# State's update by two additions over pairs of heads, and the last phase's projection weights split once and kept

## The chip, the cores and the metric

The kernel runs on one core of a Trainium2 chip. The metric is the device time of one execution in microseconds. Before the change it is 3080.32 us, the median of three runs (3077.19 to 3084.64).

Of the core's engines, the kernel uses TensorE (PE in the profile; PEld are its weight loads) for all matrix products, VectorE (DVE), ScalarE (ACT) and GpSimd (POOL) for the elementwise work, and SyncE (SP) to issue nearly all DMAs. Each engine works through its own queue in order; semaphores tie the queues together.

## The reference

One decoder block on x of 2048 tokens by 1024 channels, all in float32. A normalized and modulated input h goes through one wide projection. Its columns feed two mixers, both of which run causally over the tokens: a conv branch (gated, a depthwise convolution 31 wide, a layer norm, swish) and a rwkv branch with a matrix state of 64 x 64 for each of 16 heads. Both are gated, projected (w_conv_out, w_rwkv_out), merged by sigmoid gates, projected again (w_out), added to x and normalized.

```python
def step(state, inp):
    r_t, w_t, k_t, v_t, kk_t, b_t = inp
    sk = jnp.einsum('bhvk,bhk->bhv', state, kk_t)
    state = (state * w_t[:, :, None, :] - sk[..., None] * b_t[:, :, None, :]
             + v_t[..., None] * k_t[:, :, None, :])
    return state, jnp.einsum('bhvk,bhk->bhv', state, r_t)
...
h = _rmsnorm(x, norm_g[l]) * (1.0 + scale[:, None, :]) + shift[:, None, :]
p = jnp.einsum('bsd,de->bse', h, w_in[l])
...
m = jax.nn.sigmoid(g_conv) * y_conv + jax.nn.sigmoid(g_rwkv) * y_rwkv
out = jnp.einsum('bsd,de->bse', m, w_out[l])
x = x + gate[:, None, :] * out
```

## The kernel before

**Products by splitting.** Each large product takes float32 operands apart into a rounded high half (`hi`) and the rest (`lo`), and adds up three matmuls: hi x hi, hi x lo, lo x hi (`mm3`, L192). A weight tile is 1024 x 128, or 512 KB. `load_w` brings it in: either it loads the float32 tile (L172), rounds it on ACT (L175) and subtracts on DVE or POOL (L177), or, if both halves were written to DRAM before (`kept`), it loads the two halves (L168, L169), 512 KB each. All these tiles come from one pool of six buffers. The input projection's weights are split in the first block of tokens and kept. The weights of w_out, multiplied by the adaLN gate, are split and kept in the second block: `ogate`, by half tiles, with scratch tiles from a pool of eight (`hx`), ACT at L157 and POOL at L156 and L158. The weights of w_rwkv_out (`ro`) and w_conv_out (`co`) are not kept: `rproj` and `cproj` of the last phase load and split all eight tiles of each again for each block, on ACT and DVE.

**Stages.** The tokens run in four blocks of 512 (block 0 to 3). In each, four groups of two pairs of heads go through `group`; between its steps stand the projections for the conv branch and for the gates, each with its matmuls against h. A last phase then takes block by block: `rproj`, `cproj`, and the output projection with the residual and the final norm. For the block after, `osplit` and `lnorm` prepare the inputs: `m` or `o` tiles (hi and lo) for `rproj`, `u` tiles for `cproj`. `lnorm` ends in u on the path POOL L1024, ACT, DVE L202, DVE L1026, ACT and DVE in `split` (L911, L912).

**The state.** A block has 8 chunks of 64 tokens. A pair's step (`pair`, a generator in three parts) writes `BK`, which holds beta (L499, DVE) and k (L505, POOL) divided by the running decay, and `KR`, which holds the removal key and r times it. L518 copies BK by heads and L524 multiplies the copies with KR for the matrices within a chunk; L555 transposes BK and L556 copies it as `tk`. `pe` is the chunk's whole decay, one number for each channel and chunk. In `group`, for each chunk: ACT makes Se = S x pe (L665); TensorE applies S (L668), DVE adds (L670), TensorE solves within the chunk (L673), DVE scales (L675), TensorE sums tk with the result (L679), and DVE makes the new S as pe times that sum plus Se (L683), for two pairs by two heads in four operations of 64 x 64.

**What sets the order.** Everything is written with tiles whose waits are worked out by the language, and the instructions are put in order, on each engine and across them, by a scheduler that plays through its own estimate of each instruction's time. So an edit in one place can move instructions far from it. BK has one buffer, `tk` three, KR four.

Of the kernel before, what the change touches and what calls it, by code (L numbers as in the profile page):

```python
# [9 lines left out]
F32 = mybir.dt.float32  # L10
F32R = mybir.dt.float32r
# [7 lines left out]
P = 128  # L19
# [63 lines left out]
def hybrid_block(ctx: ExitStack, tc: tile.TileContext, x, vecs, convk, w2a2, final_g, ada, w_in, w_co, w_ro, w_o, crow, out,  # L83
# [63 lines left out]
    def ogate(n, half):  # L147

        back = kept.setdefault(("o", n), [dp.tile([P, KT, P], F32R, name=f"k{p_}_o{n[0]}_{n[1]}", tag=f"k{p_}_o{n[0]}_{n[1]}")
                                          for p_ in "hl"])  # L150
        hs = slice(half * 4, half * 4 + 4)
        st, gr, hi, lo = hx("w_st"), hx("w_gr"), hx("w_hi"), hx("w_lo")
        nc.sync.dma_start(st.rearrange("p (k n) -> p k n", k=4), wsrc["o"][n][:, hs, :])
        nc.sync.dma_start(gr[:, :256], grow_d[n[0] * 256:n[0] * 256 + 256].unsqueeze(0).broadcast_to([P, 256]))
        s4 = st.rearrange("p (k n) -> p k n", n=256)
        nc.gpsimd.tensor_tensor(out=s4, in0=s4, in1=gr[:, :256].unsqueeze(1).broadcast_to([P, 2, 256]), op=ALU.mult)  # L156
        nc.scalar.copy(hi.bitcast(F32R), st)  # L157
        nc.gpsimd.tensor_tensor(out=lo.bitcast(F32R), in0=st, in1=hi, op=ALU.subtract)  # L158
        for d_, s_ in zip(back, (hi, lo)):
            nc.sync.dma_start(d_[:, hs, :].bitcast(F32), s_.rearrange("p (k n) -> p k n", k=4))  # L160
# [283 lines left out]
    def pair(b, q_, pr, h, lora, uv, Asb, rn, res):  # L444
# [102 lines left out]
        nc.gpsimd.tensor_tensor(out=vv, in0=rk, in1=vv, op=ALU.mult)  # L547
        nc.sync.dma_start(bv_dram[b][pr], vv)

        tk = l3.tile([P, NCH, P], F32, name="tk", tag="tk", bufs=TKB)  # L550
        for c4 in range(NCH // 4):
            pt = pa.tile([P, 4, P], F32, name="aux", tag="aux")
# [7 lines left out]
    def group(b, g, h, lora, fill):  # L560
# [98 lines left out]
        for c in range(NCH):  # L659
# [18 lines left out]
            for q in range(2):  # L678
                last = nc.tensor.matmul(xo[:, 2 + q, :], R[q]["tk"][:, c, :], uv[:, c, q, :], start=False, stop=(q == 1),  # L679
                                        skip_group_check=True)  # L680
            for q, hh in heads:
                hs = slice(64 * hh, 64 * hh + 64)
                nc.vector.scalar_tensor_tensor(out=Sg[hs, q, hs], in0=xo[hs, 2 + q, hs],  # L683
                                               scalar=R[q]["pe"][hs, c:c + 1], in1=Se[hs, q, hs],
                                               op0=ALU.mult, op1=ALU.add)

        O = XO[:, 0::2]
        for c4 in range(NCH // 4):
# [170 lines left out]
    for b in range(NB):  # L859
        h = hprep(b) if b else hprep0(x0, ada_steps())  # L860
        lora = lora_split(h)
        for g in groups:
# [11 lines left out]
            if b == 1:  # L874
                for _ in range(2):
                    n_ = later.pop(0)
                    for half in range(2):
                        ogate(n_, half)

            def fill(step, n=None):  # L880
                for _ in range(n or (FILL0[step] if b == 0 and g == 0 else 0)):
# [257 lines left out]
```

## Time and profile before

| | us |
|---|---|
| median of three runs | 3080.32 |
| the profiled execution | 3079.25 |
| its span, first to last instruction | 3077.6 |
| TensorE busy in the span | 2918.8 |
| DVE busy | 2182.2 |
| POOL busy | 1161.0 |
| ACT busy | 1059.7 |
| bytes moved | 638.41 MB, mean 207 GB/s |

The four blocks of tokens run from 0 to about 650, 1235, 1830 and 2425 us, and the last phase from there. A row of stretches gives the stretch and its length, the busy time of PE, PEld, DVE, ACT and POOL with the number of instructions, the granted TensorE clock, the busy share of the DMA engines, and GB/s. A row of groups gives line, engine, operation, out<-in, shapes and count, then busy time and mean ns, and then idle time of the engine just before, with what ended it. A row of one line or tile gives shortest, median and longest duration in ns, and the first and last start. A row of waits gives who waited for what: us in total, times, longest. A row of the timeline gives start, duration and in brackets the idle time before. A row of DMA issues ends in KB each and the median us to landing.

### The profile page before, as it was taken

To read this page: it belongs to the slowest core of one execution; us is meant where nothing else is said; L and a number is where in the kernel's file an instruction comes from. 1 tells how busy PE (TensorE), PEld (TensorE's weight loads), DVE (VectorE), ACT (ScalarE), POOL (GpSimd) and SP (SyncE) were. 2 spreads that over 40 slices of the span, in tenths; PEclk is the share of its full clock that TensorE was granted. 3 is DMA by queue.
4 is the path that set the end of the run, shared out by engine and by line. 5 is a ranking of instruction groups with operands and counts; after the bars stand their busy time and mean duration, and the time that the engine had idled before them with its cause. 6 is when DMAs were issued, how large, how long until landed. Compare 5 with 4: busy or idle time off the path is not lost.

```text
span 3077.6 us, 64859 instructions
## 1 busy us (share of the span) xinstructions
PE 2918.8 (95%) x25672; PEld 2759.5 (90%) x25672; DVE 2182.2 (71%) x4199; ACT 1059.7 (34%) x1919; POOL 1161.0 (38%) x1724
## 2 busy tenths in 40 slices
PE   6799998999999999999999999999989999699998
PEld 5789998999999999999999998999989888487888
DVE  7677877787777667777768586867699465877553
ACT  4424444343324241424232323233342224343421
POOL 3355554534343434241323326345445016533100
PEclk9989999999999999999999999999989999799999
DMA  8675767664757586555646567647448658766554
GB/s 301 221 239 192 262 206 268 229 235 136 249 160 229 163 269 218 178 167 173 204 149 217 181 202 247 192 142 224 139 146 263 207 187 287 246 205 220 198 182 161
DMA packets 343327, 638.41 MB, mean 207 GB/s; under 512 B 133424, under 2 KB 152176, under 8 KB 343024
## 3 DMA queue, kind: packets, MB, share of 16 engines
q1 hardware_dynamic: 343024, 634.27, 62.8%
q8 instruction: 202, 3.31, 0.4%
q14 instruction: 101, 0.83, 0.1%
HBM read 462.10 MB, written 170.92 MB: 206 GB/s over the span
## 4 chain that ended last, share of the span: by engine, by line
PE 62%; DVE 12%; DMA 10%; POOL 7%; issue 3%; ACT 2%; SPq 2%; DVEq 0%; POOLq 0%; ACTq 0%
PE ps_main L192 43%; PE aux L524 3%; DVE acc L761 2%; DMA w_st<-w_in_t 2%; POOL TT L611 2%; POOL itmp L609 2%; PE xo L673 2%; PE pout L1061 2%; PE pout L1060 2%; PE pout L1059 2%; DMA w_lo<-kl_in 1%; PE xo L668 1%; DMA w_gr<-grow_d 1%; PE xo L679 1%; PE late L695 1%
## 5 line engine op out<-in xcount | busy, mean ns | idle before, releaser
L192 PE MATMUL ps_main<-h_hi,w_hi 128*128 128x256 f32 x4608 | 961.4, 286 | 20.4 <-ACT w_hi L175 12.2
L192 PE MATMUL ps_main<-h_hi,w_lo 128*128 128x256 f32 x4608 | 962.3, 286 | 13.6 <-POOL w_lo L177 8.0
L192 PE MATMUL ps_main<-h_lo,w_hi 128*128 128x256 f32 x4608 | 956.7, 285 | 0.0
L192 PEld LDWEIGHTS ps_main<-h_hi,w_hi 128*128 128x128 f32 x4608 | 721.7, 190 | 30.4 <-ACT w_hi L175 13.3
L192 PEld LDWEIGHTS ps_main<-h_hi,w_lo 128*128 128x128 f32 x4608 | 719.7, 190 | 21.6 <-POOL w_lo L177 10.0
L192 PEld LDWEIGHTS ps_main<-h_lo,w_hi 128*128 128x128 f32 x4608 | 719.8, 190 | 5.2 <-issue 0.5
L761 DVE SCALAR_TENSOR_TENSOR acc<-u,ck,acc 128x512 f32<-128x512 f32 x928 | 698.6, 753 | 20.0
L175 ACT CAST w_hi<-w_st 128x1024 fp32r<-128x1024 f32 x135 | 141.5, 1048 | 368.9 <-DMA w_st<-w_in_t 151.6
L683 DVE SCALAR_TENSOR_TENSOR S<-xo,pe,Se 64x64 f32<-64x64 f32 x512 | 144.6, 282 | 128.1 <-PE xo L679 118.1
L609 POOL TENSOR_TENSOR itmp<-La,TT 128x126 f32<-128x126 f32 (+22 forms) x496 | 180.7, 364 | 141.9 <-DMA La<-dA 105.9
L611 POOL TENSOR_TENSOR TT<-TT,itmp 128x126 f32<-128x126 f32 (+22 forms) x496 | 190.5, 384 | 37.2
L177 DVE TENSOR_TENSOR w_lo<-w_st,w_hi 128x1024 fp32r<-128x1024 f32 x88 | 119.5, 1359 | 103.7 <-ACT w_hi L175 47.7
L177 POOL TENSOR_TENSOR w_lo<-w_st,w_hi 128x1024 fp32r<-128x1024 f32 x47 | 113.5, 2414 | 134.5 <-ACT w_hi L175 109.0
L665 ACT ACTIVATE Se<-S,pe 128x128 f32<-128x128 f32 x256 | 89.0, 395 | 209.1 <-DVE S L683 208.0
L524 PE MATMUL aux<-KR,BKz 128*128 128x128 f32 x1024 | 138.5, 285 | 13.5 <-ACT BKz L518 8.7
L547 POOL TENSOR_TENSOR vv<-rk,vv 128x512 f32<-128x512 f32 x32 | 44.0, 1374 | 284.2 <-ACT rk L546 268.8
L524 PEld LDWEIGHTS aux<-KR,BKz 128*128 128x128 f32 x1024 | 127.6, 198 | 16.1 <-ACT BKz L518 9.1
L675 DVE TENSOR_TENSOR uv<-xo,rn 64x256 f32<-64x256 f32 x128 | 53.7, 420 | 99.8 <-PE xo L673 98.2
L741 ACT ACTIVATE th<-ps_main 128x512 f32<-128x512 f32 x64 | 38.1, 595 | 210.5 <-PE ps_main L192 157.6
L526 DVE TENSOR_TENSOR As<-aux,maskA 128x512 f32<-128x512 f32 x128 | 87.0, 688 | 27.9 <-PE aux L524 26.4
L451 POOL TENSOR_TENSOR wlo<-wf,wl 64x128 fp32r<-64x128 f32 x64 | 37.4, 584 | 173.6 <-ACT wl L448 171.1
L773 ACT ACTIVATE th<-ps_main 128x512 f32<-128x512 f32 x64 | 38.2, 597 | 184.3 <-PE ps_main L192 179.7
(298 smaller groups left out, 5489.0 us busy)
## 6 DMA issues: line engine op xcount, KB each, us to landing
w_hi<-kh_in SPq DMA_DIRECT2D x219, 512.0 KB, 4.0
w_lo<-kl_in SPq DMA_DIRECT2D x219, 512.0 KB, 5.1
w_st<-w_in_t SPq DMA_DIRECT2D x73, 512.0 KB, 5.0
kh_in<-w_hi SPq DMA_DIRECT2D x71, 512.0 KB, 2.9
kl_in<-w_lo SPq DMA_DIRECT2D x71, 512.0 KB, 4.4
w_st<-w_ro_t SPq DMA_DIRECT2D x32, 512.0 KB, 4.0
w_st<-w_co_t SPq DMA_DIRECT2D x32, 512.0 KB, 3.6
w_hi<-kh_o SPq DMA_DIRECT2D x32, 512.0 KB, 3.7
```

The lines of the kernel that those rows point to most:

```text
L175: nc.scalar.copy(hi, st)
L177: lo_eng.tensor_tensor(out=lo, in0=st, in1=hi.bitcast(F32), op=ALU.subtract)
L192: nc.tensor.matmul(ps[:, qs], ww[:, k, :], aa[k][:, qs], start=(k == 0 and t == 0 and q == 0), stop=(k == KT - 1 and t == 2 and q == ms - ...
L524: nc.tensor.matmul(pA[:, c // 2, es], BKz[:, hh, c // 2, es], KR[:, cc, es], start=(c == 0), stop=(c == 3), skip_group_check=True)
L526: nc.vector.tensor_tensor(out=Asb[:, hh, c4 * 4:c4 * 4 + 4, :].rearrange("p (a e) n -> p a (e n)", e=2), in0=pA, in1=flat(maskA).unsqueeze ...
L609: nc.gpsimd.tensor_tensor(out=tmp[:, :ni, :nt], in0=La[:, j:j + 1, j + 1:].broadcast_to([P, ni, nt]), in1=TT[:, :ni, j:j + 1].broadcast_to ...
L611: nc.gpsimd.tensor_tensor(out=TT[:, :ni, j + 1:], in0=TT[:, :ni, j + 1:], in1=tmp[:, :ni, :nt], op=ALU.add)
L665: nc.scalar.mul(Se[:, q, :], Sg[:, q, :], R[q]["pe"][:, c:c + 1])
L673: nc.tensor.matmul(xo[pr_, q, hs], As[q][pr_, hh, c, kcol(e)], XO[pr_, c, q, hs], start=(q == 0 and hh == 0), stop=(q == 1 and hh == 1), s ...
L683: nc.vector.scalar_tensor_tensor(out=Sg[hs, q, hs], in0=xo[hs, 2 + q, hs], scalar=R[q]["pe"][hs, c:c + 1], in1=Se[hs, q, hs], op0=ALU.mult ...
L761: nc.vector.scalar_tensor_tensor(out=acc if i + 1 < HALO else yj, in0=u[:, i:i + TB], scalar=ck[:, j, i:i + 1], in1=acc, op0=ALU.mult, op1 ...
L1059: nc.tensor.matmul(o_, mhi[kk][:, ts_], whi[:, k, :], start=first, stop=False, skip_group_check=True)
```

## The change

Three edits. First, after BK's last use within a chunk and before its transposes, one POOL multiplication scales all of BK (128 x 1024) by pe, so that `tk` already holds the decay. Second, the new state is then the plain sum of Se and TensorE's result, and one DVE addition serves both pairs: two operations of 64 x 128 for each chunk instead of four of 64 x 64. Third, `keep` splits the 16 tiles of w_rwkv_out and w_conv_out in block 2, four tiles at the start of each group, by half tiles on ACT and POOL like `ogate`, and stores both halves; `load_w` finds them in `kept` and loads the halves in the last phase.

```diff
+    pending = [(name, n) for name in ("ro", "co") for n in range(KT)]
+
+    def keep(name, n, half):
+        back = kept.setdefault((name, n), [dp.tile([P, KT, P], F32R, name=f"k{p_}_{name}{n}", tag=f"k{p_}_{name}{n}")
+                                           for p_ in "hl"])
+        hs = slice(half * 4, half * 4 + 4)
+        st, hi, lo = hx("w_st"), hx("w_hi"), hx("w_lo")
+        nc.sync.dma_start(st.rearrange("p (k n) -> p k n", k=4), wsrc[name][n][:, hs, :])
+        nc.scalar.copy(hi.bitcast(F32R), st)
+        nc.gpsimd.tensor_tensor(out=lo.bitcast(F32R), in0=st, in1=hi, op=ALU.subtract)
+        for d_, s_ in zip(back, (hi, lo)):
+            nc.sync.dma_start(d_[:, hs, :].bitcast(F32), s_.rearrange("p (k n) -> p k n", k=4))
...
+        BKe = BK.rearrange("p a (e n) -> p (a e) n", e=2)
+        nc.gpsimd.tensor_tensor(out=BKe, in0=BKe, in1=pe.unsqueeze(2).broadcast_to([P, NCH, 2 * CH]), op=ALU.mult)
         tk = l3.tile([P, NCH, P], F32, name="tk", tag="tk", bufs=TKB)
...
-            for q, hh in heads:
+            for hh in range(2):
                 hs = slice(64 * hh, 64 * hh + 64)
-                nc.vector.scalar_tensor_tensor(out=Sg[hs, q, hs], in0=xo[hs, 2 + q, hs],
-                                               scalar=R[q]["pe"][hs, c:c + 1], in1=Se[hs, q, hs],
-                                               op0=ALU.mult, op1=ALU.add)
+                nc.vector.tensor_tensor(out=Sg[hs, :, hs], in0=xo[hs, 2:4, hs], in1=Se[hs, :, hs], op=ALU.add)
...
+            if b == 2:
+                for _ in range(4):
+                    n_ = pending.pop(0)
+                    for half in range(2):
+                        keep(*n_, half)
```

The scheduler puts the whole program in a new order; lines of the changed kernel are 13 to 18 higher than those of the one before. Three places.

SP's queue in the last phase, at block 0's `rproj`; `rth` is a tile of the gate. Before:

```order
L172 DMA w_st<-w_ro_t 128x1024
L959 DMA rth<-gr_d_2_261 128x512
L959 DMA rth<-gr_d_3_262 128x512
L172 DMA w_st<-w_ro_t 128x1024 x2
L959 DMA rth<-gr_d_4_263 128x512
L172 DMA w_st<-w_ro_t 128x1024
```

In the changed kernel:

```order
L181 DMA w_hi<-kh_ro_16159 128x1024
L182 DMA w_lo<-kl_ro_16160 128x1024
L977 DMA rth<-gr_d_2_261 128x512
L181 DMA w_hi<-kh_ro_17986 128x1024
L182 DMA w_lo<-kl_ro_17987 128x1024
L977 DMA rth<-gr_d_3_262 128x512
L181 DMA w_hi<-kh_ro_18006 128x1024
L182 DMA w_lo<-kl_ro_18007 128x1024
```

Each tile is now two loads of the same size, with nothing of ACT or DVE behind them.

DVE's queue in the last phase, where block 1's `lnorm` works out its scale (`rv`, `dg`), with the low halves of block 2's o tiles and block 0's final norm (`xt`, `vs`, `rs`) beside it. Before:

```order
L130 SCALAR_TENSOR_TENSOR rv<-rt,rv 128x4
L177 TENSOR_TENSOR w_lo<-w_st,w_hi 128x1024
L912 TENSOR_TENSOR o_lo_33076<-ot,o_hi_33077 128x512
L1013 TENSOR_SCALAR dg<-ident,rv 128x128 x4
L912 TENSOR_TENSOR o_lo_33074<-ot,o_hi_33075 128x512
L1067 TENSOR_TENSOR xt_31909<-pout,xt_31909 128x256
L1067 TENSOR_TENSOR xt_31913<-pout,xt_31913 128x256
L1074 TENSOR_REDUCE vs<-sq_31923 128x1
L1075 TENSOR_SCALAR vs<-vs 128x1
L177 TENSOR_TENSOR w_lo<-w_st,w_hi 128x1024
```

In the changed kernel:

```order
L1085 TENSOR_TENSOR xt_31985<-pout,xt_31985 128x256
L130 SCALAR_TENSOR_TENSOR rv<-rt,rv 128x4
L128 TENSOR_TENSOR rs_t<-rs_32463 128x1
L130 SCALAR_TENSOR_TENSOR rs_32482<-rs_t,rs_32482 128x1
L1031 TENSOR_SCALAR dg<-ident,rv 128x128 x4
L129 SCALAR_TENSOR_TENSOR rs_t<-rs_t,vs 128x1
L128 TENSOR_TENSOR rs_t<-rs_32482 128x1
L130 SCALAR_TENSOR_TENSOR rs_32463<-rs_t,rs_32463 128x1
L129 SCALAR_TENSOR_TENSOR rs_t<-rs_t,vs 128x1
L128 TENSOR_TENSOR rs_t<-rs_32463 128x1
```

The two weight subtractions are gone from here, and steps of block 0's final norm stand in their place around `dg`.

POOL's queue in block 0, the scaling of a pair's BK; `s_lo` belongs to the head sums, `vv` to the bonus output, `ta` to the next pair. Before:

```order
L271 TENSOR_TENSOR s_lo<-rk,rh 128x512
L472 COPY pe<-E_4871 128x8
L177 TENSOR_TENSOR w_lo<-w_st,w_hi 128x1024
L547 TENSOR_TENSOR vv<-rk,vv 128x512
L177 TENSOR_TENSOR w_lo<-w_st,w_hi 128x1024
L503 TENSOR_TENSOR ta<-ta,k 128x512
```

In the changed kernel:

```order
L485 COPY pe<-E_4843 128x8
L564 TENSOR_TENSOR BK<-BK,pe 128x1024
L190 TENSOR_TENSOR w_lo<-w_st,w_hi 128x1024
L560 TENSOR_TENSOR vv<-rk,vv 128x512
L190 TENSOR_TENSOR w_lo<-w_st,w_hi 128x1024
L516 TENSOR_TENSOR ta<-ta,k 128x512
```

The scaling stands ahead of a weight split of the first block, of `vv` and of the next pair's work.

## The prediction

> **What bounds the kernel now.** I read the busy shares first, then the same shares by stage: the four token blocks (0, 650, 1235, 1830 us) and the last phase from 2425.
>
> ```profile
> PE 2918.8 (95%) x25672; PEld 2759.5 (90%) x25672; DVE 2182.2 (71%) x4199; ACT 1059.7 (34%) x1919; POOL 1161.0 (38%) x1724
> 0.00:650.00 650.00, 578.19 (x5284) 556.17 (x5285) 478.64 (x904) 260.63 (x439) 309.79 (x425) 0.96 0.71 239
> ...
> 1235.00:1830.00 595.00, 590.65 (x5752) 574.93 (x5751) 434.76 (x884) 197.00 (x377) 186.05 (x365) 1.00 0.57 183
> 1830.00:2425.00 595.00, 579.10 (x5634) 558.86 (x5633) 439.99 (x835) 189.67 (x339) 269.44 (x421) 0.98 0.61 196
> 2425.00:3078.00 653.00, 596.03 (x3386) 511.39 (x3385) 401.18 (x721) 213.51 (x382) 171.11 (x116) 0.95 0.63 210
> ```
>
> TensorE bounds the four blocks: in block 2 it idles 4 us of 595. The change takes no matmul away, so only its idle time and its slow-clock time can be won, and most of those lie in the last phase. Cutting that phase finer finds the place.
>
> ```profile
> 2550.00:2575.00 25.00, 20.68 (x148) 19.73 (x148) 10.62 (x19) 6.96 (x17) 16.92 (x14) 0.86 0.97 356
> 2575.00:2600.00 25.00, 25.00 (x214) 25.00 (x214) 11.89 (x25) 9.60 (x25) 19.69 (x15) 1.00 0.81 271
> 2600.00:2625.00 25.00, 14.84 (x70) 11.30 (x68) 24.72 (x45) 10.11 (x19) 20.58 (x15) 0.90 0.49 166
> 2625.00:2650.00 25.00, 23.72 (x94) 18.93 (x95) 24.95 (x43) 14.97 (x21) 10.32 (x5) 0.89 0.97 335
> 2650.00:2675.00 25.00, 10.99 (x31) 7.69 (x30) 21.22 (x24) 3.75 (x5) 15.12 (x11) 0.72 0.84 266
> 2675.00:2700.00 25.00, 19.76 (x62) 14.56 (x62) 12.44 (x14) 7.90 (x11) 14.45 (x10) 0.73 0.50 160
> ```
>
> From 2600 to 2675 DVE is full (24.7, 25.0 and 21.2 us of each 25) while TensorE idles and its granted clock (third column from the right) drops to 0.72. This is block 1's pair of projections, rwkv then conv. TensorE's waits in 2600 to 2700, and the rows that bracket them:
>
> ```profile
> PE ps_main L192 <- DVE rs L125: 10.8, 1, 10.8
> PE ps_main L192 <- ACT w_hi L175: 10.8, 2, 6.2
> PE ps_main L192 <- DVE w_lo L177: 8.5, 3, 4.1
> 2604.34 0.39 PE L192 MATMUL ps_main<-m_lo,w_hi 128*128 128x512 f32 x1
> 2623.72 1.21 DVE L177 TENSOR_TENSOR w_lo<-w_st,w_hi 128x1024 fp32r<-128x1024 f32 x1
> 2626.84 0.63 PE L192 MATMUL ps_main<-m_lo,w_hi 128*128 128x512 f32 x1
> 2627.27 0.63 PE L192 MATMUL ps_main<-m_hi,w_lo 128*128 128x512 f32 x1
> L1059 PE MATMUL pout<-w_hi,m_hi x256: 277/281/283, 2737.7 to 3066.4; 128*128 128x256 f32 x128
> 2932.28 89.61 PE ps_main L192 x384
> ```
>
> The two projections run from 2604.0, one matmul before the fourth row, to 2737.7, where the output projection's first matmul of the m tiles stands: 133.7 us. The last row, from the chain of waits, is block 3's pair: the same 384 matmuls without a wait in 89.6 us, 0.233 apart; after a stall they start 0.43 apart (the rows at 2626.84 and 2627.27). Of the 44 us between, 30.1 are the waits above, all for weight splits: I count the 10.8 under "rs" too, since w_lo stood in DVE's queue behind those square-root steps and ended at 2624.9. The remaining 14 are mostly the slow clock.
>
> **Part 1, the kept weights, last phase.** Per projection tile, 64 times, ACT's rounding and DVE's subtraction go away and a 512 KB load becomes two.
>
> ```profile
> L175 ACT CAST w_hi<-w_st 128x1024 fp32r<-128x1024 f32 x135 | 141.5, 1048 | 368.9 <-DMA w_st<-w_in_t 151.6 <-DMA w_st<-w_co_t 84.3 <-DMA w_st<-w_ro_t 66.3
> L177 DVE TENSOR_TENSOR w_lo<-w_st,w_hi x88: 1209/1225/2364, 91.2 to 3010.5; 128x1024 fp32r<-128x1024 f32 x88
> L177 DVE TENSOR_TENSOR w_lo<-w_st,w_hi 128x1024 fp32r<-128x1024 f32 x7 | 9.6, 1368 | 0.0
> L912 DVE TENSOR_TENSOR u_lo<-y,u_hi x8: 677/682/1699, 2632.5 to 2670.7; 128x512 fp32r<-128x512 f32 x8
> ```
>
> 64 x 1.05 = 67 us of ACT and 64 x 1.225 = 78 us of DVE, by the median, leave. What is late next is the conv projection's input u, whose last low half starts at 2670.7 and ends at 2672.4. The third row is the DVE subtractions between 2598 and 2671, seven, 9.6 us, ahead of it in a full queue. So u is whole at about 2662.8, and the rwkv projection, no longer waiting, ends at 2604 + 44.8 = 2649. The conv projection's first tile waits for u, its other seven need 7 x 24 x 0.233 = 39.2, and that wait costs some 3.5 of slow clock (14 us of wait, after which about 7 run at half speed): it ends at 2662.8 + 1 + 39.2 + 3.5 = 2706.5 instead of 2737.7, a gain of 31. Bounds: 22 if u comes no earlier (2672.4 + 1 + 39.2 + 3.5 = 2716), 43 if u is never waited for (2604 + 89.6 + 1.5 for small matmuls between = 2695). I take 30. The loads' cover is two whole tiles, 2 x 24 x 0.233 = 11.2 us, since six buffers now hold three pairs; a 512 KB load of a kept half takes about 5 (first row):
>
> ```profile
> w_lo<-kl_in SPq DMA_DIRECT2D x219, 512.0 KB, 5.1
> PE ps_main L192 <- DVE mr L962: 4.3, 2, 3.7
> PE pout L1059 <- DMA w_hi<-kh_o: 3.9, 1, 3.9
> ```
>
> The second row is block 2's rwkv projection waiting for DVE to empty PSUM; relieved by some subtractions, 1 of the 4.3 (0 to 4). The last is the only wait of the output projections for kept halves.
>
> **Part 2, splitting them once, in block 2.** 32 half tiles, each a load, an ACT rounding, a POOL subtraction and two stores, given out four tiles at the start of each group.
>
> ```profile
> L158 POOL TENSOR_TENSOR w_lo<-w_st,w_hi 128x512 fp32r<-128x512 f32 x16 | 20.7, 1292 | 8.3 <-ACT w_hi L157 8.0
> L157 ACT CAST w_hi<-w_st 128x512 fp32r<-128x512 f32 x16 | 9.9, 621 | 52.7 <-POOL w_st L156 47.5 <-DMA gc_d<-th 5.2
> PE ps_main L192 <- DMA w_lo<-kl_in: 2.9, 2, 2.5
> ```
>
> 32 x 1.29 = 41 us on POOL (busy 186 of 595), 32 x 0.62 = 20 on ACT (197 of 595), 96 transfers of 256 KB = 25 MB, so SP's queue goes from 183 to about 225 GB/s, under block 0's 239. TensorE's work covers all of it unless a store that waits for POOL holds a weight load behind it on SP: block 1, which splits 16 halves of w_out, lost 2.9 us that way (last row, the waits of that block alone). I take +3, bounds 0 and 8.
>
> **Part 3, the state's update.** Per chunk, four DVE operations become two.
>
> ```profile
> L683 DVE SCALAR_TENSOR_TENSOR S<-xo,pe,Se 64x64 f32<-64x64 f32 x512 | 144.6, 282 | 128.1 <-PE xo L679 118.1 <-ACT t L419 1.6
> L675 DVE TENSOR_TENSOR uv<-xo,rn 64x256 f32<-64x256 f32 x128 | 53.7, 420 | 99.8 <-PE xo L673 98.2
> L526 DVE TENSOR_TENSOR As<-aux,maskA 128x512 f32<-128x512 f32 x128 | 87.0, 688 | 27.9 <-PE aux L524 26.4
> PE xo L679 <- DVE uv L675: 4.7, 6, 1.5
> PE xo L673 <- DVE XO L670: 4.0, 4, 1.4
> PE xo L668 <- DVE S L683: 3.7, 5, 1.1
> ```
>
> An addition of 64x128 is not in the trace; two-input PSUM operations cost 420 ns at 256 columns and 688 at 512, 1.05 per column, so about 285 at 128 (bounds 226, the shortest of L683, and 420). 512 x 0.282 = 145 us become 256 x 0.285 = 73: 72 us of DVE, 0.56 per chunk. It is no path: DVE waits 118 us for TensorE there, TensorE waits 3.7 for S. The three waits of the chain are 12.4 together; I take -4, bounds 0 and -12.
>
> **Part 4, scaling beta and k.** One POOL multiplication of 128x1024 for each of 32 pairs; the nearest rows:
>
> ```profile
> L721 POOL TENSOR_TENSOR XO<-XO,grs 128x1024 f32<-128x1024 f32 x16 | 31.1, 1942 | 70.0 <-DVE grs L130 56.4 <-ACT h_hi L351 13.5
> L177 POOL TENSOR_TENSOR w_lo<-w_st,w_hi x47: 2340/2395/2772, 16.2 to 651.0; 128x1024 fp32r<-128x1024 f32 x47
> PE ps_main L192 <- POOL w_lo L177: 8.0, 7, 2.2
> ```
>
> L721 also reads a broadcast operand, so 2.0 us (bounds 1.9 and 2.4), 32 x 2.0 = 64 us of POOL. It waits for ACT's copies of BK (L518); behind it queue vv, weight splits and ta, and the transposes into tk (L555) wait for it. In blocks 1 to 3 projections cover that. In block 0 TensorE already waits 8.0 us for POOL's splits (third row), and in three of its eight pairs the scaling now stands directly ahead of one: +3, bounds 0 and 16.
>
> By the Trainium skill, "SBUF — State Buffer", section "Who interferes with whom", a DVE instruction with two SBUF inputs contends with a GpSimd instruction that reads SBUF. L177's 1209 ns at least and 2364 at most agree. That speaks against the change: 105 added us of POOL reads would, each holding one DVE operation for its whole length, return more than the 72 us of DVE that the state edit frees; the sum, by TensorE's waits, would stay.
>
> **Sum.** -30 - 1 + 3 - 4 + 3 = -29. The profiled execution took 3079.25 (span 3077.6 and 1.65 around it): 3050. The median, 3080.32, lies 1.1 higher: **3051**.
>
> **Rivals.** *The loads become the wait.* The rows from 2600 to 2700 moved 25 us x (166 + 335 + 266 + 160) = 23.2 MB. Eleven tiles' second halves add 5.8: 29.0 MB. At the best row's 356 GB/s (share 0.97) that takes 81 us, so 19 of the 30 stay: 3062; at 313, midway to the 271 row, 93 us, and 7 stay: 3074. For it: two rows are already at 0.97. Against: the output projection streams 1 MB per 5.6 us with one wait of 3.9 us. I put it at 3067.
>
> The skill's "DMA: Bandwidth & Descriptors", "Specifications", gives about 358 GB/s of HBM per core, and the 356 row agrees; "HBM Reference", "Specifications", says a core alone reaches about 425, by which (29.0/425 = 68 us, an estimate) this rival would vanish. No row here exceeds 356.
>
> *POOL's scaling is exposed (slower).* BK has one buffer: the next pair's writes of it (L499, L505) wait for the transposes, and these for the scaling. At x us per pair exposed on TensorE the time is 3080.3 - 32 + 32x; it is slower by over 0.2% from x = 1.2, and at 1.5 it is 3096, at the full 2.0 3112. For: POOL's order, where it stands ahead of splits and of vv. Against: TensorE idles 4 us in block 2 and 16 in block 3 now, so 10 us a block would have to be new.
>
> *More is freed.* u not waited for (-43) and the state's bound of -12: 3080.3 - 43 - 1 + 3 - 12 + 3 = 3030.
>
> *It moves nothing.* The splits' waits turn fully into waits for u and loads: 3080.
>
> **How the numbers follow.** Forecast 3051 (3036 to 3062) 0.50; loads 3067 0.20; exposed scaling 3096 0.14; more freed 3030 0.12; nothing moved 0.04. The range, 3022 to 3084, leaves out most of the slower case and the lowest edge. 0.2% is about what a measurement of this kernel tells from no change. Faster: 0.50 + 0.12 + 0.14 of the loads' 0.20 = 0.76; same: 0.06 + 0.04 = 0.10; slower 0.14.
>
> **What would show it.** Right: the waits for w_hi and w_lo gone from the last phase; block 1's two projections in about 103 us rather than 133.7, with u as their one wait and the clock above 0.85; 256 additions of about 285 ns; 32 scalings near 2 us; blocks 0 to 3 ending within 10 us of 2425. Wrong: waits for loads of kept halves there, or TensorE waiting for tk, BK or w_lo in the four blocks.

## The result

The changed kernel takes 3063.56 us, median of 5 runs (3056.37 to 3072.41), against 3080.32 us (3077.19 to 3085.61). The ratio is 0.9945, 95% interval 0.9927 to 0.9963: about 17 us faster, where 29 were forecast. The profiled execution took 3056.37 us (span 3054.7), the fastest of the five, and that matters below.

The same marks as before cut it into stages: lead-in, the four blocks (each from its first low-rank matmul), and the last phase from the first matmul of the rwkv projection. The kernel before was profiled a second time for comparison. The columns are span; busy us and count of PE, PEld, DVE, ACT and POOL; granted clock; DMA share; GB/s. First the second profile of the kernel before (all its stages stand in the table of stages below):

```profile
69.30:686.00 616.70, 573.66 (x5369) 552.33 (x5368) 457.16 (x835) 246.57 (x413) 294.27 (x403) 0.96 0.70 232
...
1274.80:1853.00 578.20, 574.69 (x5634) 559.37 (x5633) 420.12 (x857) 190.12 (x365) 184.34 (x365) 1.00 0.57 183
...
2445.00:3079.50 634.50, 578.39 (x3242) 494.40 (x3240) 391.16 (x702) 207.09 (x371) 171.30 (x116) 0.95 0.63 211
```

and the changed kernel:

```profile
69.20:691.30 622.10, 573.68 (x5369) 554.08 (x5367) 457.79 (x785) 246.79 (x413) 309.20 (x411) 0.96 0.69 230
691.30:1280.90 589.60, 575.93 (x5606) 559.44 (x5605) 407.91 (x791) 198.47 (x384) 238.91 (x404) 0.99 0.64 203
1280.90:1864.70 583.80, 578.25 (x5660) 562.63 (x5659) 411.84 (x793) 206.98 (x397) 238.65 (x404) 1.00 0.69 225
1864.70:2449.70 585.00, 568.02 (x5505) 548.98 (x5503) 414.37 (x752) 184.42 (x336) 281.64 (x427) 0.99 0.61 198
2449.70:3054.70 605.00, 574.47 (x3250) 490.67 (x3248) 304.56 (x634) 143.35 (x308) 167.01 (x116) 0.97 0.77 275
```

The last phase is shorter by 27 to 30 us, with the same TensorE work at a clock of 0.97 instead of 0.95. The blocks give a part of it back: 5.5 us more in block 0, about 1 to 4 in block 1, 3 to 6 in block 2, and 7 to 10 less in block 3.

In the last phase, what is left of TensorE's waits (columns: total us, times, longest):

```profile
PE ps_main L205 <- DVE mr L980: 7.9, 4, 3.8
PE pout L1077 <- DMA w_hi<-kh_o: 3.9, 1, 3.9
PE ps_main L205 <- DMA w_lo<-kl_ro: 3.9, 4, 1.2
PE ps_main L205 <- DMA w_hi<-kh_ro: 1.8, 2, 1.1
...
PE ps_main L205 <- DMA w_hi<-kh_co: 0.4, 1, 0.4
```

All waits for a weight being split are gone. The wait for the conv input u, which the prediction expected here, is 0.2 us. The two that took their place are DVE's emptying of PSUM (mr, line 980; 962 before) and the loaded halves. The rows that bracket block 1's pair of projections, the low halves of its u, and the changed operations:

```profile
L205 PE MATMUL ps_main<-m_hi,w_hi x128: 388/395/794, 2608.6 to 2952.8; 128*128 128x512 f32 x128
L1077 PE MATMUL pout<-w_hi,m_hi x256: 277/281/363, 2720.7 to 3043.5; 128*128 128x256 f32 x128
L930 DVE TENSOR_TENSOR u_lo<-y,u_hi x8: 684/691/1175, 2641.7 to 2682.4; 128x512 fp32r<-128x512 f32 x8
L698 DVE TENSOR_TENSOR S<-xo,Se 64x128 f32<-64x128 f32 x256 | 73.5, 287 | 107.6 <-PE xo L694 96.9 <-PE aux L570 5.5 <-issue 2.4
L564 POOL TENSOR_TENSOR BK<-BK,pe 128x1024 f32<-128x1024 f32 x32 | 61.4, 1918 | 67.5 <-DVE As L539 37.9 <-ACT BKz L531 20.9 <-DVE ss L130 7.3
L171 POOL TENSOR_TENSOR w_lo<-w_st,w_hi 128x512 fp32r<-128x512 f32 x32 | 42.5, 1329 | 93.0 <-ACT w_hi L170 92.1 <-DMA kl_ro<-w_lo 0.8
```

The pair takes 2720.7 - 2608.6 = 112.1 us instead of 133.7; 103 were forecast, 89.6 is the pair without a wait. The new operations last as long as estimated (287 ns for 285, 1.92 us for 2.0). In lines 564 and 171 the figure behind the last bar is idle time of POOL in front of them: 67 and 93 us, which no term of the prediction contains.

### The profile page after: what moved, and what is told of

It is laid out like the page before. It is cut to its first block, busy times and chain, and to the rows that moved or that the text cites. A ratio compares the mean times of both kernels' runs of the same rounds, so it can differ in the third digit from the quotient of the medians.

```text
span 3054.7 us, 64810 instructions
## 1 busy us (share of the span) xinstructions
PE 2911.1 (95%) x25672; PEld 2754.0 (90%) x25672; DVE 2045.2 (67%) x3879; ACT 1010.8 (33%) x1887; POOL 1257.3 (41%) x1788
## 4 chain that ended last, share of the span: by engine, by line
PE 57%; DMA 15%; DVE 12%; POOL 7%; ACT 3%; issue 3%; SPq 2%; DVEq 0%; ACTq 0%; POOLq 0%
PE ps_main L205 40%; DMA w_st<-w_in_t 3%; PE aux L537 3%; DVE acc L774 2%; POOL TT L626 2%; POOL itmp L624 2%; DMA w_gr<-grow_d 2%; DMA w_st<-w_co_t 2%; PE xo L688 2%; PE pout L1078 2%; PE pout L1079 2%; PE pout L1077 2%; DMA w_st<-w_ro_t 1%; PE xo L683 1%; PE xo L694 1%
## 5 line engine op out<-in xcount | busy, mean ns | idle before, releaser
L205 PE MATMUL ps_main<-h_hi,w_hi 128*128 128x256 f32 x4608 | 953.4, 285 | 24.3 <-ACT w_hi L188 16.1
L698 DVE TENSOR_TENSOR S<-xo,Se 64x128 f32<-64x128 f32 x256 | 73.5, 287 | 107.6 <-PE xo L694 96.9
L188 ACT CAST w_hi<-w_st 128x1024 fp32r<-128x1024 f32 x71 | 74.3, 1047 | 195.9 <-DMA w_st<-w_in_t 159.3
L685 DVE TENSOR_TENSOR XO<-xo,XO 128x256 f32<-128x256 f32 x128 | 53.7, 419 | 86.1 <-PE xo L683 70.1
L531 ACT COPY BKz<-BK 64x512 f32<-64x512 f32 x128 | 78.9, 616 | 62.7 <-PE aux L537 39.7
```

What stands on the lines that cost most here:

```text
L188: nc.scalar.copy(hi, st)
L205: nc.tensor.matmul(ps[:, qs], ww[:, k, :], aa[k][:, qs], start=(k == 0 and t == 0 and q == 0), stop=(k == KT - 1 and t == 2 and q == ms - ...
L531: nc.scalar.copy(BKz[hs, hh], BK[hs, c4 * 2:c4 * 2 + 2])
L698: nc.vector.tensor_tensor(out=Sg[hs, :, hs], in0=xo[hs, 2:4, hs], in1=Se[hs, :, hs], op=ALU.add)
```

## The experiments

Each kernel was timed against the kernel before on the same chip. "Kept alone" is the kept projection weights without the state's edit, "state alone" the reverse. The two kernels "no scaling" leave the decay out of the state's sum, so their states are not the reference's; they serve for their times alone.

| kernel | median us | kernel before, us | ratio (95%) |
|---|---|---|---|
| changed | 3063.56 | 3080.32 | 0.9945 (0.9927 to 0.9963) |
| changed, again | 3068.27 | 3077.52 | 0.9960 (0.9946 to 0.9974) |
| kept alone | 3065.52 | 3077.52 | 0.9952 (0.9935 to 0.9970) |
| state alone | 3089.87 | 3077.52 | 1.0040 (1.0023 to 1.0057) |
| split in block 2, not used | 3086.02 | 3077.72 | 1.0025 (1.0014 to 1.0035) |
| state alone, no scaling | 3078.23 | 3077.99 | 0.9997 (0.9984 to 1.0009) |
| changed, no scaling | 3059.42 | 3077.72 | 0.9942 (0.9926 to 0.9957) |
| changed, scaling on DVE | 3079.15 | 3077.99 | 1.0007 (0.9994 to 1.0020) |
| changed, root batched | 3067.20 | 3077.52 | 0.9955 (0.9939 to 0.9970) |
| changed, norm spread | 3058.50 | 3077.99 | 0.9936 (0.9921 to 0.9950) |
| the same, scaling earlier | 3057.74 | 3077.72 | 0.9937 (0.9921 to 0.9953) |
| kept alone, norm spread | 3056.26 | 3077.72 | 0.9929 (0.9914 to 0.9944) |

The lengths of the stages, one profile each, cut at the same marks (us):

```
                          block 0  block 1  block 2  block 3  last phase
before                     616.5    585.6    580.9    595.2     631.8
before, again              616.7    588.8    578.2    592.0     634.5
changed                    622.1    589.6    583.8    585.0     605.0
changed, again             630.7    588.8    587.0    587.5     607.0
changed, root batched      627.9    590.4    592.9    585.1     602.7
changed, norm spread       621.9    595.7    590.0    587.3     599.4
kept alone                 617.5    583.9    592.8    596.9     605.7
split, not used            611.0    584.4    591.0    592.2     622.6
state alone                619.0    593.8    580.5    592.3     625.8
kept alone, norm spread    616.6    585.8    593.7    593.1     595.0
norm spread, sc. earlier   623.8    591.3    595.2    586.4     595.3
state alone, no scaling    625.3    591.3    577.2    596.4     630.3
changed, no scaling        619.1    590.9    586.6    592.2     597.5
changed, scaling on DVE    621.5    592.2    588.2    596.9     611.1
```

### How far one profile can be trusted: both kernels once more

No edit; for the kernel before, empty lines alone.

> The changed kernel once more, as it is. It gives a second profile and a second set of times: if block 1's two projections again take 110 to 114 us and the waits for DVE's evacuation (about 8 us) and for the loaded halves (about 11 us) are there again, these are the kernel's and not that one execution's. Time 14 to 22 us under the kernel before.

> The kernel before, with empty lines added, for a second profile of it. If the 616.6 us of its block 0 and the 631.8 us of its last phase are the kernel's and not that execution's, the second profile has them within 4 us; the granted clock's half-speed stretches in block 0 would be about 48 us again.

The kernel before repeated its stages within 4 us (3081.16 us in all). The changed kernel, at 3068.27 us, gained 9 us rather than the 14 to 22 expected, though the intervals of the two ratios overlap. Its last phase repeated (607.0), as did its block 1 pair (2732.2 - 2620.9 = 111.3 us), the mr wait (10.4 us) and the kept halves (2.5 + 4.9 us of ro's). Its block 0 did not:

```profile
69.10:699.80 630.70, 577.64 (x5369) 557.65 (x5368) 459.10 (x785) 247.15 (x413) 310.97 (x411) 0.95 0.68 227
...
2463.10:3070.10 607.00, 572.65 (x3249) 489.17 (x3248) 307.66 (x634) 143.01 (x308) 163.38 (x116) 0.98 0.77 274
```

The same program spent 8.6 us more in block 0, at a clock of 0.95 instead of 0.96. So its first profile was a lucky one: "blocks 0 to 3 within 10 us" held there (2449.7 against 2445.8) and failed here (2463.1). Four profiles have the changed kernel's blocks 0 to 3, with the same operations in the same order on every engine (changed, again, root batched, norm spread). They average 625.7, 591.1, 588.4 and 586.2 us; the two of the kernel before average 616.6, 587.2, 579.6 and 593.6: +9, +4, +9 and -7, **+15 in all where the prediction had +2**. The last phase's 606 against 633 is -27, where it had -31.

### Which part gains, which part pays: each alone

```diff
# kept alone: the state's update as before, and no scaling
-        nc.gpsimd.tensor_tensor(out=BKe, in0=BKe, in1=pe..., op=ALU.mult)
-                nc.vector.tensor_tensor(out=Sg[hs, :, hs], in0=xo[hs, 2:4, hs], in1=Se[hs, :, hs], op=ALU.add)
+                nc.vector.scalar_tensor_tensor(out=Sg[hs, q, hs], ... scalar=R[q]["pe"][hs, c:c + 1], ...)
# state alone
-            if b == 2:
-                for _ in range(4):
-                    ... keep(*n_, half)
```

> The kernel before with the kept projection weights alone; the state is updated as before and nothing is scaled on POOL. Theory A (the whole gain lies in the last phase and the kept weights make it; the state's edit gives a little back in blocks 0 to 3): the last phase runs as in the changed kernel, block 1's two projections in 108 to 116 us instead of 133.7, block 2's in 95 to 98 instead of 100.8, and the whole is 18 to 30 us under the kernel before, so level with the changed kernel or up to 8 us faster. Rival B (the state's edit pays a part of the gain): 8 to 15 us under the kernel before, that is 5 us or more slower than the changed kernel.

> The kernel before with the two additions per step and the scaling of beta times k on POOL alone; the projection weights are split in the last phase as before. Theory A: within 0.2% of the kernel before, more likely 1 to 6 us slower, the last projections beginning 0 to 8 us later and the last phase unchanged (block 1's two projections 130 to 137 us). Rival B: 5 to 12 us faster than the kernel before.

Kept alone is level with the changed kernel of the same chip (3065.5 and 3068.3), though its ratio's 15 us fall short of the 18 to 30 expected. Its last phase is the changed kernel's (605.7). State alone is 12 us **slower** than the kernel before, more than expected, and the opposite of rival B. So the whole gain is the kept weights', and the state's edit pays nothing over the whole. The parts don't add up, though: by the ratios -15 and +12 would be -3, and the changed kernel has -12 and -17 in its two sets, just outside what the intervals allow.

### What the splitting costs

```diff
         back = kept.get((name, n))
-        if back is not None:
+        if back is not None and name not in ("ro", "co"):
```

This stands on kept alone.

> The kernel before, with the splitting and storing of the 16 projection tiles in block 2 added, but the last phase loads and splits the weights again as before; the state is updated as before. It pays for the splitting and gets nothing for it. The prediction priced the splitting at 3 us (0 to 8). Theory G (the splitting takes about what was predicted): 0 to 6 us slower than the kernel before, block 2 in 580 to 586 us. Rival H (block 2's 592.8 us in the run with the kept weights alone is the splitting's price): 8 to 14 us slower, block 2 in 589 us or more.

It is 8 us slower by the medians, 4 to 11 by the interval: above theory G's 6, at the lower edge of theory H, and above the 3 us of the prediction. Block 2 is as theory H has it, at 591.0, 592.8 and 593.7 us in the three kernels that have the splitting and the old state, against 578.2 and 580.9. This run's own profile is its lowest time (3072.35 us, its last phase and block 0 shorter than before by 9 and 6 us), so the other stages of it say little. TensorE's waits in block 2 of this kernel:

```profile
PE ps_main L205 <- DMA w_lo<-kl_in: 2.5, 4, 1.6
PE aux L570 <- ACT uv L554: 1.9, 2, 1.1
PE xo L688 <- DVE XO L685: 1.6, 3, 1.2
...
PE aux L505 <- ACT sq L501: 1.3, 1, 1.3
PE ps_main L205 <- DVE th L758: 1.3, 1, 1.3
```

In the second profile of the kernel before that block has only three waits, 3.3 us together (w_lo<-kl_in, XO and S); here twelve add up to 13.4. Of the 10 us more, loaded weights have 1.7; the rest are for ACT, DVE and POOL. Line 170, ACT's rounding of a half, shows where they can come from. The waits of ACT and POOL in that block:

```profile
POOL w_lo L171 <- ACT w_hi L170: 91.3, 24, 8.9
...
ACT w_hi L170 <- DMA w_st<-w_co_t: 43.6, 12, 6.8
ACT w_hi L170 <- DMA w_st<-w_ro_t: 23.0, 9, 6.2
```

and the piece of ACT's timeline ahead of a uv that TensorE waited for, with SP's issue of the load first (start, length, what, idle time before it):

```profile
1573.21 0.42 SPq L169 DMA_DIRECT2D w_st<-w_ro_t  x1
...
1578.80 0.62 ACT L170 CAST w_hi<-w_st 128x512 fp32r<-128x512 f32 x1 [4.82 <-issue]
1579.32 1.17 ACT L554 COPY uv<-aux 64x512 f32<-64x512 f32 x2
1580.51 0.58 ACT L559 COPY rk<-aux 128x512 f32<-128x512 f32 x1
```

The profile names no releaser for the 4.82 us, but the load was issued at 1573.21, and the loads of these halves take 5.0 us to land (median), which is about when the rounding starts. It stands in ACT's queue before its load has landed, so ACT stands still with uv and rk behind it: 66.6 us in all, for the halves of both weights, in the waits that name the load. POOL stands still behind ACT for 91 us. The prediction priced 20 us of ACT and 41 us of POOL as busy time, which TensorE's work does cover. It did not price what these waits hold up. That uv was late for this reason is read from the order of these rows; no run took the waits alone away.

### What the state's edit costs, and where

```diff
# state alone, no scaling (and the same edit on the changed kernel)
-        nc.gpsimd.tensor_tensor(out=BKe, in0=BKe, in1=pe..., op=ALU.mult)
-                nc.vector.tensor_tensor(out=Sg[hs, :, hs], in0=xo[hs, 2:4, hs], in1=Se[hs, :, hs], op=ALU.add)
+                nc.vector.scalar_tensor_tensor(out=Sg[hs, :, hs], in0=xo[hs, 2:4, hs], scalar=0.02, in1=Se[hs, :, hs],
+                                               op0=ALU.mult, op1=ALU.add)
# changed, scaling on DVE
-        nc.gpsimd.tensor_tensor(out=BKe, ...)
+        nc.vector.tensor_tensor(out=BKe, ...)
```

> The kernel before with the state's update over the pairs, two operations a step, but no scaling on POOL: the update multiplies by the constant 0.02 in place of the decay, so that the state's values are not the reference's. The projection weights are split in the last phase as before. Theory E (the scaling is what costs): level with the kernel before or up to 8 us faster, that is 10 to 20 us under the state's edit with its scaling (3089.87 us). Rival F (the shorter update with its other order costs by itself): 3084 us or more.

> The changed kernel without the scaling on POOL: the state's update over the pairs multiplies by the constant 0.02 in place of the decay, so that the state's values are not the reference's. The kept weights are as in the changed kernel. Theory E (the scaling costs 12 us wherever it is, as between the two runs of the state's edit with and without it): 8 to 14 us faster than the changed kernel, ratio to the kernel before 0.991 to 0.9925. Rival I (the 12 us belong to the order of instructions that the state's edit alone got, and the changed kernel has another): within 4 us of the changed kernel, ratio 0.994 to 0.997.

> The changed kernel with the scaling of beta times k on DVE instead of POOL, at the same place. Theory E (what the state's edit costs in blocks 0 to 3 is POOL's queue, longer by 32 operations of 1.9 us, behind which KR and the transposes of beta times k wait): waits for POOL's KR and for the scaled tile fall from 6.2 us to under 3, blocks 0 to 3 end 5 to 12 us earlier, the whole is 5 to 12 us faster than the changed kernel. Rival F (the cost is the chain itself, one more operation ahead of the transposes wherever it runs, or another order of the instructions altogether): within 4 us of the changed kernel, or slower.

Two operations instead of four, without the scaling, are level with the kernel before: 0.9997. The 72 us of DVE that they free show no gain (the interval, 0.9984 to 1.0009, could hide 5 us), and with the scaling the kernel is 12 us slower, as theory E says. In the changed kernel, taking it out gives 0.9942 against 0.9945 and 0.9960: rival I, between 1 and 6 us, not separable from nothing. And moving it to DVE makes the changed kernel 11 to 16 us slower by the medians, which is against theory E and with rival F (the edit also gives the instructions another order from block 0 on). There the marked wait did go down, and others went up by more. The changed kernel first:

```profile
PE xo L683 <- DVE S L698: 9.0, 7, 3.0
...
PE aux L537 <- POOL KR L523: 6.2, 3, 3.5
...
PE xo L694 <- DVE uv L690: 4.5, 4, 2.1
...
PE xo L688 <- DVE XO L685: 2.3, 5, 0.6
```

With the scaling on DVE:

```profile
PE xo L683 <- DVE S L698: 11.4, 10, 3.0
...
PE xo L688 <- DVE XO L685: 6.6, 10, 1.2
PE xo L694 <- DVE uv L690: 6.3, 6, 2.1
...
PE aux L537 <- POOL KR L523: 2.2, 1, 2.2
```

KR's wait falls from 6.2 to 2.2, the three of the state's chain grow from 15.8 to 24.3, and the wait for ACT's copies of BK grows from 4.2 to 9.0. The 3.5 us wait for KR is itself not a long POOL operation: in the changed kernel KR stands in POOL's queue behind the multiplication of a w_out half whose gate row has not landed.

```profile
1161.07 1.30 POOL L518 TENSOR_TENSOR BK<-ta,E 128x512 f32<-128x512 f32 x1
1166.09 1.26 POOL L156 TENSOR_TENSOR w_st<-w_st,w_gr 128x512 f32<-128x512 f32 x1 [3.72 <-DMA w_gr<-grow_d]
1167.31 1.18 POOL L523 TENSOR_TENSOR KR<-r,E 128x512 f32<-128x512 f32 x1
```

POOL idles 3.72 us for that row while TensorE waits for KR. In the kernel before KR was not behind such a wait: it followed BK directly.

```profile
1149.43 1.30 POOL L505 TENSOR_TENSOR BK<-ta,E 128x512 f32<-128x512 f32 x1
1150.68 1.63 POOL L510 TENSOR_TENSOR KR<-r,E 128x512 f32<-128x512 f32 x1
```

The state's edit touches neither line; it gave the instructions another order, and in this order an old wait reached TensorE. All traces agree: TensorE waits for KR in every kernel with two operations, whether the scaling is on POOL (3.2 to 6.7 us), on DVE (2.2) or left out (3.7 and 4.2), and in none with four.

The stages say the same. Until the splitting begins in block 2, state alone has on every engine the order of the changed kernel, and kept alone that of the kernel before. Blocks 0 and 1 together take 1195 to 1206 us in the five profiles with four operations and 1212 to 1220 in the six with two and the scaling on POOL, so there the state's edit costs about 14 us, with the kept weights and without. Without the scaling they still take 1217 us (the slowest execution of its kernel) and 1210 (the fastest of its), and TensorE's queue has the same order in these blocks as with it. So most of the 14 us goes with the order that the two operations bring, not with the scaling's time on POOL. From block 2 on state alone and the changed kernel differ: beside the kept weights blocks 2 and 3 take 588 and 586 us instead of 593 and 595, which gives the 14 back; alone they take 581 and 592 instead of 580 and 594.

**Left open:** why the edit gains in blocks 2 and 3 only beside the kept weights, and where state alone without the scaling, level over the whole, wins back what it loses in blocks 0 and 1 (its profile, 3092.58 us, is 14 us over its median). The profile of state alone is its second fastest execution (3082.51 us, median 3089.87), so its trace holds little of the 12.

### What still bounds block 1's projections

```diff
# root batched: one 128x4 reciprocal root for the four token tiles of a block
-            for tt in range(NTT):
-                finish(tt)
+            vs4 = ...; rs4 = ...
+            rsqrt(rs4, vs4, ...)
+            (eight scalings of xt by rs4[:, tt] as before)
# norm spread: the same root, and scaling n made to wait for mr[n], inside rproj
+                nc.vector.scalar_tensor_tensor(out=rg, in0=mr[n][:, 0:1], scalar=0.0, in1=rs4[:, tt:tt + 1], ...)
+                nc.vector.scalar_tensor_tensor(out=xts[tt][n % 2], in0=xts[tt][n % 2], scalar=rg, in1=fg[:, hs], ...)
```

> The changed kernel, with the final normalisation of blocks 0 to 2 written so that the reciprocal root of all four token tiles is made at once on a 128x4 tile: 12 small DVE operations a block in place of 4 times 12. Theory C (DVE's queue, full of these small operations beside POOL's work, makes the evacuation of block 1's first projections late): the waits for DVE's mr in block 1's projections fall from 7.9 us to under 2, block 1's two projections take 100 to 107 us instead of 112.1, and the whole is 5 to 10 us faster than the changed kernel. Rival D (the loads of the kept halves bound this stretch, and DVE's wait only stands in front of theirs): the wait moves to the weights' halves, and the whole is within 3 us of the changed kernel.

> The changed kernel, with the final normalisation of blocks 0 to 2 spread over the next block's first projection: the reciprocal root at once on 128x4, and of the eight scalings of xt one behind each evacuation of mr, which it is made to wait for by a 128x1 operation that reads the evacuated tile. Theory C (what makes the evacuation late is DVE's queue: the scalings of xt stand ahead of it and are slow beside POOL): the waits for DVE's mr in the last phase fall from 7.9 us (13.0 us with the root batched alone) to under 3 us, the last phase takes 594 to 600 us instead of 605, and the whole is 4 to 10 us faster than the changed kernel. Rival D (the loads of the kept halves bound this stretch): mr's waits go and the loads' waits grow by as much, the last phase within 3 us of 605.

The timeline of the changed kernel in block 0's normalisation, POOL's row first, then DVE's and TensorE's (start, length, what, number of operations):

```profile
2618.26 11.28 POOL L1042 TENSOR_TENSOR y<-y,rl 128x512 f32<-128x512 f32 x8
...
2620.08 3.38 DVE L1098 SCALAR_TENSOR_TENSOR xt<-xt,rs,fg 128x512 f32<-128x512 f32 x2
...
2623.44 0.67 DVE L980 SCALAR_TENSOR_TENSOR mr<-rth,ps_main 128x512 f32<-128x512 f32 x1
...
2624.64 1.20 DVE L129 SCALAR_TENSOR_TENSOR rs_t<-rs_t,vs 128x1 f32<-128x1 f32 x1
2625.76 0.15 DVE L128 TENSOR_TENSOR rs_t<-rs 128x1 f32<-128x1 f32 x1
...
2624.17 0.79 PE L205 MATMUL ps_main<-m_hi,w_hi 128*128 128x512 f32 x1 [3.38 <-DVE mr L980]
```

TensorE waited 3.38 us for that mr (last row). While POOL multiplies, every second DVE operation on one column takes 1.20 us and the one after it 0.15, and two scalings of xt take 3.38 (two later ones, 1.40). Batching the root took the small operations away, and the wait grew to 13.0 us: the expectation was wrong, and the time, 3067.2 us, is the changed kernel's. The scalings stood ahead of mr as one piece instead, here in block 2's pair, where 5.3 of the 13.0 us fall:

```profile
2784.43 8.55 DVE L1126 SCALAR_TENSOR_TENSOR xt<-xt,rs,fg 128x512 f32<-128x512 f32 x8
2792.90 0.67 DVE L980 SCALAR_TENSOR_TENSOR mr<-rth,ps_main 128x512 f32<-128x512 f32 x1
```

Putting one scaling behind each evacuation brought mr's wait to 3.8 us (expected under 3), the last phase to 599.4 us (594 to 600), and the time to 3058.5 us, 5 to 10 us under the changed kernel by the medians (the intervals of their ratios overlap; the second set below, 3057.7 us, is as low). Theory C holds so far as it says that the normalisation in DVE's queue makes mr late. The eight scalings of xt are enough for it, as the batched root shows; in the second profile of the changed kernel, of whose 10.4 us one wait has 8.2, small operations fill the first 5 us of that wait and two scalings the next 2.4. A part of rival D shows too: waits for the co halves rose from 0.9 to 5.0 us.

```profile
PE ps_main L205 <- DVE mr L980: 3.8, 1, 3.8
PE ps_main L205 <- DMA w_hi<-kh_co: 3.2, 3, 2.5
PE ps_main L205 <- DMA w_lo<-kl_co: 1.8, 3, 0.9
```

### Two more versions with the spread normalisation

Scaling of beta times k earlier: its two lines in the source moved from behind the value's transposes to ahead of them. Kept alone with the spread normalisation: the two edits above together.

> The changed kernel with the final normalisation spread, and the scaling of beta times k issued on POOL right after the products that still need it unscaled, ahead of the value's transposes instead of behind them. If the wait for the scaled tile ahead of its transposes (2.6 us in block 1 with the spread normalisation) is what the scaling costs, that wait goes and the whole is 2 to 8 us under 3058.5 us. If POOL's queue is what costs, it stays within 3 us of it or gets slower, since KR's waits stay.

> Kept weights and the final normalisation spread behind the evacuations, without the state's edit. If the spread normalisation is worth its 5 to 10 us here too, and the state's edit is worth nothing beside the kept weights (the kept weights alone stood within 3 us of the changed kernel), this is 3054 to 3061 us, level with the changed kernel with the spread normalisation (3058.5 us). If the state's edit gains with the kept weights, it is 4 us or more slower than that.

The earlier scaling tested neither theory. The scheduler put the scaling where it stood: the two traces have the same operations in the same order on every engine. So its 3057.7 us and its last phase of 595.3 us are a second set of the spread normalisation (3058.5 and 599.4). Kept alone with the spread normalisation is the fastest of all, 3056.26 us, with a last phase of 595.0 us; it can't be told from the two with the state's edit (0.9929 against 0.9936 and 0.9937). The kept weights and the spread normalisation are so worth 21 us against the kernel before, and the state's edit can be left out. Against the changed kernel this is 7 to 12 us by the medians, clear of the interval of one of its two sets.

## Why the prediction was right or wrong

The sign and the place were right: 3063.6 and 3068.3 us lie in 3022 to 3084, and the gain is in the last phase. The forecast of 3051 had 12 to 17 us too much of it, and both sets lie outside its own 3036 to 3062. By the profiles the miss is 4 us in the last phase (-27 for -31) and 13 in blocks 0 to 3 (+15 for +2). By its steps:

- **Part 1, -30, and -1 for mr.** Measured -27 in the last phase. All waits for w_hi and w_lo are gone, and 64 subtractions of DVE. But the step from which the 30 was worked out failed: "the conv projection's first tile waits for u", with u whole 59 us after the pair's start instead of 68, and the rwkv projection ending 45 us after it. Measured from the pair's start, u was whole after 74.5 us, later than before, and the rwkv projection took 62 (61 in the second profile). TensorE did not wait for u even so: it ran the 18 matmuls of the first tile for which u was there, went on to the next tile, and left those of u's last two parts (whole at 2680.0 and 2683.1) for later. The 17 us are in the rwkv projection itself: 7.2 of the mr wait, 3.5 of the ro halves, the rest mostly a clock of 0.84 around them. The pair gained 22 us in both profiles, the prediction's lower bound, though not by the wait for u from which that bound was worked out; some 5 us more came in the rest of the phase, where the sum had 1. That -27 comes so near to -31 is in part luck. The mr term had the wrong sign: it went from 4.3 to 7.9 instead of losing 1, because with the weight splits gone the normalisation was what stood ahead of it in DVE's queue.
- **Part 2, +3 (0 to 8).** Mis-sized: 8 measured over the whole, 13 in block 2 with the old state (592.5 against 579.6, averages) and 9 with the new. Busy times were right (0.62 and 1.33 us). "TensorE's work covers all of it unless a store that waits for POOL holds a weight load" looked at SP's queue; by the order of the rows it was ACT and POOL that held other work behind loads that had not landed.
- **Part 3, -4 (0 to -12).** The 285 ns were right, the gain was about 0 (0.9997; the interval does not exclude the 4). "It is no path" was the correct reading, and the -4 was taken beside it without a row that shows it: the wait for S rose from 3.7 to 9.0 us.
- **Part 4, +3 (0 to 16).** 1.92 us for 2.0; 12 us if the edit stands alone, 1 to 6 in the changed kernel. In the changed kernel blocks 0 and 1 pay 13 us and block 3 gains 7, and most of the 13 is there without the scaling too. So the sum priced the scaling's time and left out what a new order of the instructions does, such as the waits for KR. The rival "exposed scaling" needed 1.2 us a pair to make the whole slower; 12 us over 32 pairs are 0.4.
- **Contention.** By the Trainium skill, "SBUF — State Buffer", "Who interferes with whom", a DVE operation with two SBUF inputs contends with a GpSimd operation that reads SBUF; the prediction set POOL's whole 105 us of added reads against DVE. The rule's direction agrees (the 1.20 us above). The size is far smaller: DVE is busy 2125.1 us in state alone and 2109.8 without the scaling, 2045.2 in the changed kernel and 2033.5 without it, so the scaling's 61 us of POOL return 12 to 15 us of DVE. Over the whole change DVE's busy time fell by 137 us, from 2182.2 to 2045.2, where the edits remove 64 x 1.225 + 144.6 - 73.5 = 150 at the subtractions' median.
- **The rival of the loads, 3067.** Near the measured time, by another way: kept ro and co halves cost 6.6 us of waits in the last phase, which the prediction had named as a sign of being wrong. Its limit of 356 GB/s was not one, as the rows below show.

## What to carry to other kernels

Price an operation that waits for a load by what stands behind it in its engine's queue, not by its busy time: 20 us of work on an ACT that was busy for a third of the block came with 8 us of TensorE's time. When work is taken off a full engine, look for what that engine does next ahead of the result that others wait for; here it was a normalisation whose output nobody needed yet. Where a scheduler stands between the source and the queues, look whether an edit reached them: moving the scaling's lines gave the same queues, and two operations for four gave an order that cost 14 us in two blocks. And profile a kernel twice before giving a stage 5 us: the same program's block 0 took 622 and 631 us.

## What the runs showed of the hardware

- **Loads faster than the best row of before.** Block 1's projections in the changed kernel (windows, columns as above):

```profile
2625.00:2650.00 25.00, 21.02 (x73) 15.91 (x72) 23.19 (x40) 9.84 (x16) 8.81 (x7) 0.84 0.78 264
...
2645.00:2695.00 50.00, 44.89 (x180) 32.56 (x179) 27.57 (x35) 11.15 (x19) 22.10 (x16) 1.00 1.04 397
```

  397 GB/s over 50 us, with one core running, where the prediction's rival took 356 as the limit. Of the two pages it set against each other, the Trainium skill's "HBM Reference", "Specifications (TRN2)" (about 425 alone) is the one that this agrees with; "DMA: Bandwidth & Descriptors", "Specifications" (about 358) is exceeded.
- **One-column DVE operations beside POOL.** While POOL runs 128x512 multiplications of 1.4 us (11.28 / 8), they take 1.20 and 0.15 us in turn, so two of them cost about 1.3 us instead of 0.3. Why every second one passes unhindered these rows don't show.
- **The spread of one kernel's times goes with the granted clock.** Of the second set of the changed kernel, the fastest, 3060.98 us, had 0.982, the slowest, 3077.11, had 0.977; a line through time and clock of the 33 runs of the kernel before beside it falls by 2.8 us for each 0.001 (correlation -0.68); in the two other sets of the kernel before it falls by 1.8 and 1.9. What sets the clock from run to run these runs don't show.
